# Retention's group norm in a hybrid trunk: roots on compact token sums, outputs in the banks of w_out's last token tile

## The chip, the cores and the metric

One NeuronCore of a Trainium2 chip runs the whole program. The metric is the device time of one execution in microseconds (us); three executions of the kernel before are given, and one more was profiled.

## The reference

The program is one inference step of a two-layer trunk over 384 tokens: 128 prompt tokens and 256 sample tokens, width 1024. Each layer normalises and modulates its input, runs four mixers beside each other (retention, Hyena, windowed attention, latent attention) on one combined input projection, joins their outputs with `w_out`, normalises again, and then runs a gated MLP. All matrices are float32.

What the change touches is the end of the retention mixer and the start of the product with `w_out`:

```python
o = o_f + jnp.flip(o_b, 2)                       # per head: 64 values for each token
mu = jnp.mean(o, axis=-1, keepdims=True)
var = jnp.var(o, axis=-1, keepdims=True)
o = ((o - mu) * lax.rsqrt(var + EPS)).transpose(0, 2, 1, 3).reshape(b, seq_len, RET_WIDTH)
y = jax.nn.silu(gate.astype(jnp.float32)) * (o * gn_g.astype(jnp.float32))
...
y = jnp.concatenate([y_ret, y_hy, y_gqa, y_mla], axis=-1) @ p['w_out']
```

Four heads of 64 channels make 256 channels. Each token has one root per head, so 384 x 4 roots are needed per layer.

## The kernel before

**Layout.** Activations lie with channels on partitions and tokens on the free axis. The 384 tokens are three tiles of 128: tile 0 is the prompt, tiles 1 and 2 the samples. Retention works on two pairs of heads (`pr` = 0, 1); a pair fills 128 partitions, 64 for each head. Wide products are made in three passes: each float32 operand is cut into a rounded upper part (ACT, line 355) and a lower part (DVE, or GpSimd where `eng=G` is given, line 356), and upper x upper, upper x lower and lower x upper are summed in one bank. These passes are the lines 1236 to 1238 for `w_out`.

**PSUM.** There are eight banks: two of tag "a", five of tag "m", one of tag "n". A bank is given to a tile when the planner places its first instruction, and passes on when all users of the tile before are done.

**Retention's tail** (`retention`, lines 1190 to 1226), for each pair: scores of samples against samples into two "a" banks (line 1196), times the decay tables (`W`, line 1199), then the outputs `o` of all 384 tokens into one "a" bank (lines 1204, 1207, 1211). Values and states were made mean-free before, so `o` has mean zero and only its variance is left. It is squared on ACT (1214), summed over the 64 channels of each head and spread back to all 128 partitions by one product with the block matrix `bd` into a second "a" bank `rvp` (1216). The root (ACT, 1217), the reciprocal and one Newton step (DVE, 1218 to 1221) work on 128 x 384 values, in which each root stands 64 times. Then DVE multiplies by the gate (1223) and by `o` and the gain `gn` (1224), and the result is cut into upper and lower parts (`mix`). The second pair needs both "a" banks for its scores, and these are held by the first pair's `o` and `rvp`.

**The product with w_out.** `acc` has six banks: three token tiles times two halves of 512 columns. `mixout[k]`, k = 0 to 7, are the eight 128-channel slices of the mixers' outputs; k = 0 and 1 are retention's two pairs. The weights of k = 6, 7, 4 are multiplied first for all three tiles (18 matmuls for each k). The weights of k = 5, 2, 3 go into the same three buffers (`wh`) that hold those of 6, 7, 4, so each is cut when an earlier one has been read for the last time; those of k = 0, 1 and of the MLP's first two units `up_w` have buffers of their own (`wq`). Then `out_part(t, h)`, steps `ma` and `mb` of token tile t, adds k = 5, 2, 3 for both halves (18 matmuls) and k = 0, 1 for half h (6 matmuls). Steps `q`, `y`, `b`, `r`, `n`, `x` are the norm and residual of a tile, `s` to `i` the next norm, the transposes (`ta`, `tv`, line 759) and the modulation. Their order on PE, DVE and ACT is written out by hand in `OUT_ORDER` (first layer) and `OUT_LAST_ORDER` (second layer, where `tv0` stands ahead of `ma2`).

**What sets the order around the change.** Retention and the early part of `w_out` aren't ordered by hand on PE, DVE and ACT: a planner with a cost for each instruction simulates the engines and puts the earliest in the program's order that is ready next. On the chip each engine then runs that fixed order. On SP the block's loads keep their order: weights of k = 6, 7, 4, 5, 2, 3, 0, 1, then `up_w`, then the gates `gg`; other loads, such as those of `x`, may be placed between. A weight load needs one of five `raw` buffers, which is free when both parts have been cut from it.

Of the kernel before, what the change touches and what calls it, by code (L numbers as in the profile page):

```python
# [9 lines left out]
F32 = mybir.dt.float32  # L10
# [4 lines left out]
ALU = mybir.AluOpType  # L15
# [69 lines left out]
def _consts():  # L85
    p = np.arange(128)
    c0, c, cf = {}, {}, {}
    c0["ident"] = np.eye(128)
    perm = np.zeros((128, 128))
    perm[p ^ 32, p] = 1.0  # L90
    c["perm"] = perm
    c["iup"] = np.broadcast_to(np.arange(1, 257)[None], (128, 256))
    cos, sin = _rope(256, 64)
    c["rc"] = np.tile(np.concatenate([cos, cos], 1).T, (2, 1))
    c["rs"] = np.tile(np.concatenate([-sin, sin], 1).T, (2, 1))
    cos, sin = _rope(256, 32)
    mt = np.zeros((128, 256))
    mt[64:96] = np.concatenate([cos, cos], 1).T
    mt[96:128] = np.concatenate([-sin, sin], 1).T
    c["mrope"] = mt  # L100
    kc = np.concatenate([cos, cos], 1).reshape(2, 128, 32).transpose(1, 0, 2)
    ks = np.concatenate([-sin, sin], 1).reshape(2, 128, 32).transpose(1, 0, 2)
    c["kc"] = kc.reshape(128, 64)
    c["ks"] = ks.reshape(128, 64)
    w256 = (2 * np.arange(256) + 1) * np.pi / 512
    w128 = (2 * np.arange(128) + 1) * np.pi / 256
    a = np.outer(p + 0.5, w256)
    c["fc"] = np.cos(a)
    c["fs"] = -np.sin(a)
    c["ic"] = np.cos(a).T.reshape(2, 128, 128).transpose(1, 0, 2).reshape(128, 256)  # L110
    c["is"] = np.sin(a).T.reshape(2, 128, 128).transpose(1, 0, 2).reshape(128, 256)
    a = np.outer(p, w128)
    c["pfc"] = np.cos(a)
    c["pfs"] = -np.sin(a)
    c["bd"] = np.where(p[:, None] // 64 == p[None, :] // 64, 1.0 / 64, 0.0)
    c["pic"] = np.cos(a).T
    c["pis"] = -np.sin(a).T
    m0 = np.where(p[None, :] <= p[:, None], 0.0, -1e30)
    m1 = np.where(p[None, :] >= p[:, None], 0.0, -1e30)
    zs, ts = _zfeat(256)  # L120
    zp, tp = _zfeat(128)
    col = np.zeros((128, 16))
    col[:, 0:3] = np.stack([-tp, -ts[:128], -ts[128:]], 1)
    for b, (w, L) in enumerate(((w256[:128], 256), (w256[128:], 256), (w128, 128))):
        col[:, 3 + 3 * b] = np.cos(w / 2) / L
        col[:, 4 + 3 * b] = np.sin(w / 2) / L
        col[:, 5 + 3 * b] = -np.cos(w / 2) / L
    col[:, 12] = 127 - p
    col[:, 13] = p
    col[:, 14] = EPS  # L130
    c0["col"] = col
    a3 = np.zeros((128, 3))
    a3[64:, 0] = 1.0
    a3[:64, 2] = 1.0
    c0["addc"] = a3
    m = np.arange(256)
    a = np.outer(m + 0.5, w256)
    cf["gc"] = np.cos(a).reshape(2, 128, 256).transpose(1, 0, 2).reshape(128, 512)
    cf["gs"] = np.sin(a).reshape(2, 128, 256).transpose(1, 0, 2).reshape(128, 512)
    a = np.outer(p + 0.5, w128)  # L140
    cf["gpc"] = np.cos(a)
    cf["gps"] = np.sin(a)
    z = np.zeros((17, 384))
    z[:, 0:128] = zp.T
    z[:, 128:384] = zs.T
    return c0, c, cf, {"z": z, "mask": np.concatenate([m0, m1], 1), "lag": np.arange(384)[None, :] - 128 - p[:, None]}
# [122 lines left out]
def trunk(ctx: ExitStack, tc: tile.TileContext, A, O, offs, depth=DEPTH):  # L269
# [76 lines left out]
    def bank(tag="a", name="bk"):  # L346
        kw = {"bufs": 1} if tag == "n" else {}
        return (pa if tag == "a" else pm).tile([128, 512], F32, tag=tag, name=name, **kw)
# [771 lines left out]
    def retention(l, mx, M, P_, rt, hi, lo, tma):  # L1120
# [8 lines left out]
        for src, dst, n in ((v4, vcn.rearrange("p t (h e) -> p t h e", h=4), 12), (s0, s0c.rearrange("p (a e) -> p a e", a=4), 4)):  # L1129
            mu = sm.tile([128, 12], F32, tag="rmu", name="rmu", bufs=1)[:, 0:n]  # L1130
            m = mu.rearrange("p (t h) -> p t h", t=3) if n == 12 else mu
            V.tensor_reduce(out=m, in_=src, op=ALU.add, axis=AX.X)
            V.tensor_scalar(mu, mu, 1.0 / 64, None, ALU.mult)
            V.tensor_tensor(out=dst, in0=src, in1=m.unsqueeze(3 if n == 12 else 2).to_broadcast(list(dst.shape)), op=ALU.subtract)
        q, k, sg = [], [], []
        for j in range(6):
            ps = fm_proj(l, 9 + j, hi, lo)
# [3 lines left out]
                (q if j < 2 else k).append(f)  # L1141
            else:
                th = mx.tile([128, TP], F32, tag="w15", name="rth", bufs=11)
                S.activation(out=f, in_=ps[:, 0:TP], func=ACTF.Copy, scale=0.5)
                S.activation(out=th, in_=ps[:, 0:TP], func=ACTF.Tanh, scale=0.5)
                V.scalar_tensor_tensor(out=f, in0=th, scalar=1.0, in1=f, op0=ALU.add, op1=ALU.mult)
                sg.append(f)
# [38 lines left out]
            W0.append(M(("wuk", "wuv")[b]).rearrange("p (a c) -> p a c", a=2))  # L1186
            V.tensor_tensor(out=W0[b], in0=pc[b][:, 0:256].rearrange("p (a c) -> p a c", a=2), in1=tabs[:, :, b, 128:256], op=ALU.mult)
        s4 = s0c.rearrange("p (a b e) -> p a b e", a=2, b=2)
        gn = P_("gn")
        for pr in range(2):  # L1190
            sc = [bank("a", "rsc") for _ in range(2)]
            W = [mx.tile([128, 2, 256], F32, tag="PT", name="rW", bufs=3) for _ in range(2)]
# [4 lines left out]
            for b in range(2):  # L1197
                for j in range(2):
                    V.tensor_tensor(out=W[b][:, j], in0=sc[b][:, 256 * j:256 * j + 256],
                                    in1=tab[:, 2 * pr + b, 128 - 128 * j:384 - 128 * j], op=ALU.mult)  # L1200
            o = bank("a", "rob")
            hs = [slice(64 * (2 * pr + b), 64 * (2 * pr + b) + 64) for b in range(2)]
            for b in range(2):
                T.matmul(o[64 * b:64 * b + 64, 0:128], vcn[:, 0, hs[b]], W0[b][:, pr], start=True, stop=True)
# [5 lines left out]
                    r = slice(64 * b, 64 * b + 64)  # L1210
                    T.matmul(o[r, 128:384], s4[r, pr, dr], qd[r, pr, dr], start=False, stop=(dr == 1))

            sq, y, u = (mx.tile([128, 384], F32, tag="w15", name=n, bufs=11) for n in ("rsq", "rya", "ru"))
            S.activation(out=sq, in_=o[:, 0:384], func=ACTF.Square)
            vp = bank("a", "rvp")[:, 0:384]
            T.matmul(vp, cc("bd"), sq, start=True, stop=True)
            S.activation(out=y, in_=vp, func=ACTF.Sqrt, bias=col(14))
            V.reciprocal(y, y)
            V.tensor_tensor(out=u, in0=y, in1=y, op=ALU.mult)
            V.scalar_tensor_tensor(out=u, in0=vp, scalar=EPS, in1=u, op0=ALU.add, op1=ALU.mult)  # L1220
            V.scalar_tensor_tensor(out=y, in0=u, scalar=-3.0, in1=y, op0=ALU.add, op1=ALU.mult)
            for x0, x1, g0 in ((0, 128, 0), (128, 384, 130)):
                V.scalar_tensor_tensor(out=y[:, x0:x1], in0=y[:, x0:x1], scalar=-0.5, in1=sg[pr][:, g0:g0 + x1 - x0], op0=ALU.mult, op1=ALU.mult)
            V.scalar_tensor_tensor(out=y, in0=o[:, 0:384], scalar=gn[:, pr:pr + 1], in1=y, op0=ALU.mult, op1=ALU.mult)
            a, b_ = mix_tiles(pr)
            split(y, a[:, 0:384], b_[:, 0:384])

# [91 lines left out]
    for l in range(depth):  # L1319
# [4 lines left out]
        with ExitStack() as ph:  # L1324
# [76 lines left out]
            wqc = tc.tile_pool(name="wq", reuse_waits="tile", bufs=4, side="right")  # L1401
            wq = wqc.__enter__()
            gg = gate_tiles(wq)
            acc = banks6("acc")
            with tc.manual_schedule(engines={mybir.EngineType.SP}):
                for j, k in enumerate((6, 7, 4)):
                    down_step(acc, wunit(A["wout"][l, k]), mixout[k], T0, j == 0, False)
                ws = [(wunit(A["wout"][l, k]), mixout[k]) for k in (5, 2, 3)]
                ws += [(wunit(A["wout"][l, k], 1024, wq), mixout[k]) for k in (0, 1)]
                up_w = [wunit(A["wup"][l, u], 1024, wq, eng=G) for u in (0, NF)]  # L1410
                for r in range(2):
                    gate_load(gg, 2 * (l % 2), r)
        vec1, vec2 = vecs[l, 1], vecs[l, 2]
# [147 lines left out]
```

## Time and profile before

| | us |
|---|---|
| median of 3 runs | 1109.37 |
| lowest, highest | 1106.87, 1114.67 |
| the profiled execution's own time | 1114.31 |
| its span in the trace | 1112.5 |

| engine | busy us | share |
|---|---|---|
| PE | 1083.0 | 97% |
| PEld (weight loads, beside PE) | 899.1 | 81% |
| DVE | 676.0 | 61% |
| ACT | 499.9 | 45% |
| POOL | 75.3 | 7% |

PE is TensorE, DVE is VectorE, ACT is ScalarE, POOL is GpSimd, SP issues the DMAs. A timeline row gives the start in us from the span's start, the duration in us, the engine, the line, the operation with what it writes and reads, its shape, how many were merged, and in brackets the idle time before it with what ended it. The busy time of a PE row includes the pipeline's end, so the spacing of matmuls is read from their starts. A row of the chain of waits has start, us, and the instruction. The mean granted clock of the whole run is 0.987 of TensorE's full 2.4 GHz.

### The profile page before, as it was taken

To read this page: it belongs to the slowest core of one execution; us is meant where nothing else is said; L and a number is where in the kernel's file an instruction comes from. 1 tells how busy PE (TensorE), PEld (TensorE's weight loads), DVE (VectorE), ACT (ScalarE), POOL (GpSimd) and SP (SyncE) were. 2 spreads that over 40 slices of the span, in tenths; PEclk is the share of its full clock that TensorE was granted. 3 is DMA by queue.
4 is the path that set the end of the run, shared out by engine and by line. 5 is a ranking of instruction groups with operands and counts; after the bars stand their busy time and mean duration, and the time that the engine had idled before them with its cause. 6 is when DMAs were issued, how large, how long until landed. Compare 5 with 4: busy or idle time off the path is not lost.

```text
span 1112.5 us, 15627 instructions
## 1 busy us (share of the span) xinstructions
PE 1083.0 (97%) x5779; PEld 899.1 (81%) x5779; DVE 676.0 (61%) x1465; ACT 499.9 (45%) x1099; POOL 75.3 (7%) x82
## 2 busy tenths in 40 slices
PE   9999999997899999999999999999799999999997
PEld 3596767665699999999987786787589999999996
DVE  6858954477785545455565666658666454554554
ACT  6655534242764433334465544533366343343433
POOL 3210000002200000000002000001220000000000
PEclk9999999998999999999999999999889999999999
DMA  9765345856555333334337615461616434333301
GB/s 348 239 247 163 133 151 201 301 203 227 190 198 169 133 133 114 133 114 132 110 122 244 231 65 183 162 218 42 207 51 198 147 117 131 116 124 131 125 19 57
DMA packets 53017, 176.12 MB, mean 158 GB/s; under 512 B 8618, under 2 KB 10538, under 8 KB 52429
## 3 DMA queue, kind: packets, MB, share of 16 engines
q1 hardware_dynamic: 49229, 171.26, 44.9%
q10 hardware_dynamic: 3712, 3.87, 1.0%
q8 instruction: 45, 0.74, 0.3%
q14 instruction: 31, 0.25, 0.1%
HBM read 169.66 MB, written 5.44 MB: 157 GB/s over the span
## 4 chain that ended last, share of the span: by engine, by line
PE 90%; DVE 7%; ACT 2%; issue 1%; DMA 0%; DVEq 0%; ACTq 0%
PE ups L380 6%; PE gps L380 6%; PE gps L382 6%; PE ups L382 6%; PE gps L381 6%; PE ups L381 6%; PE facc L1236 5%; PE facc L1238 5%; PE facc L1237 5%; PE adaps L404 4%; PE fmps L380 4%; PE fmps L382 4%; PE fmps L381 4%; PE acc L1236 2%; PE acc L1237 2%; PE acc L1238 2%
## 5 line engine op out<-in xcount | busy, mean ns | idle before, releaser
L356 DVE TENSOR_TENSOR wlo<-raw,whi 128x512 fp32r<-128x512 f32 (+2 forms) x380 | 257.2, 706 | 215.7 <-ACT whi L355 215.4
L355 ACT CAST whi<-raw 128x512 fp32r<-128x512 f32 (+2 forms) x388 | 221.4, 610 | 282.6 <-PE gps L381 97.8
L1236 PE MATMUL facc<-whi,fah 128*128 128x512 f32 x264 | 104.5, 396 | 0.5 <-ACT fah L355 0.5
L1237 PE MATMUL facc<-wlo,fah 128*128 128x512 f32 x264 | 103.9, 394 | 0.0
L1238 PE MATMUL facc<-whi,fal 128*128 128x512 f32 x264 | 103.8, 395 | 0.0
L380 PE MATMUL gps<-hTa,whi 128*128 128x386 f32 (+4 forms) x184 | 62.4, 339 | 0.0
L380 PE MATMUL ups<-hTa,whi 128*128 128x386 f32 (+4 forms) x184 | 62.3, 339 | 0.0
L380 PE MATMUL gps<-hTb,whi 128*128 128x386 f32 (+4 forms) x184 | 62.3, 339 | 0.0
L380 PE MATMUL ups<-hTb,whi 128*128 128x386 f32 (+4 forms) x184 | 61.6, 335 | 0.6 <-ACT hTb L772 0.6
L381 PE MATMUL ups<-hTb,whi 128*128 128x386 f32 (+4 forms) x184 | 61.4, 334 | 0.8 <-POOL hTb L775 0.8
L382 PE MATMUL gps<-hTa,wlo 128*128 128x386 f32 (+4 forms) x184 | 62.1, 337 | 0.0
L381 PE MATMUL ups<-hTa,whi 128*128 128x386 f32 (+4 forms) x184 | 61.9, 336 | 0.0
L381 PE MATMUL gps<-hTa,whi 128*128 128x386 f32 (+4 forms) x184 | 61.9, 336 | 0.0
L381 PE MATMUL gps<-hTb,whi 128*128 128x386 f32 (+4 forms) x184 | 61.8, 336 | 0.0
L382 PE MATMUL gps<-hTb,wlo 128*128 128x386 f32 (+4 forms) x184 | 61.8, 336 | 0.0
L382 PE MATMUL ups<-hTa,wlo 128*128 128x386 f32 (+4 forms) x184 | 61.8, 336 | 0.0
L382 PE MATMUL ups<-hTb,wlo 128*128 128x386 f32 (+4 forms) x184 | 61.5, 334 | 0.0
L404 PE MATMUL adaps<-araw,cs 128*32 128x512 f32 x384 | 60.2, 602 | 0.0
L1238 PEld LDWEIGHTS facc<-whi,fal 128*128 128x128 f32 x264 | 49.6, 188 | 11.9
L1236 PEld LDWEIGHTS facc<-whi,fah 128*128 128x128 f32 x264 | 49.6, 188 | 10.8 <-ACT fah L355 0.9
L1237 PEld LDWEIGHTS facc<-wlo,fah 128*128 128x128 f32 x264 | 49.6, 188 | 9.9
L1236 PE MATMUL acc<-whi,mix 128*128 128x512 f32 x96 | 41.1, 434 | 11.8 <-ACT mix L355 11.8
(366 smaller groups left out, 2340.9 us busy)
## 6 DMA issues: line engine op xcount, KB each, us to landing
araw<-in_ada_dram SPq DMA_DIRECT2D x96, 512.0 KB, 4.4
raw<-in_wup_dram SPq DMA_DIRECT2D x88, 512.0 KB, 3.3
raw<-in_wdn_dram SPq DMA_DIRECT2D x44, 512.0 KB, 3.2
raw<-in_win_dram SPq DMA_DIRECT2D x30, 512.0 KB, 4.4
raw<-in_wout_dram SPq DMA_DIRECT2D x16, 512.0 KB, 5.2
gg<-gd SPq DMA_DIRECT2D x8, 512.0 KB, 5.8
raw<-in_wta_dram SPq DMA_DIRECT2D x8, 416.0 KB, 3.3
x<-in_x_dram SPq DMA_DIRECT2D x6, 512.0 KB, 6.7
```

Source lines behind the costliest of these rows:

```text
L355: S.copy(hi, src)
L356: (eng or V).tensor_tensor(out=lo, in0=src, in1=hi, op=ALU.subtract)
L380: T.matmul(out, ah, bh, start=start, stop=False)
L381: T.matmul(out, ah, bl, start=False, stop=False)
L382: T.matmul(out, al, bh, start=False, stop=stop)
L404: T.matmul(self.ps[32 * j:32 * j + 32, :], cs[:, k, :], rows[j // 2][:, 512 * (j % 2):512 * (j % 2) + 512], start=(k == self.k0), stop=(k ...
L1236: T.matmul(acc[t][h], ah[:, cs_], wh_[:, hs], start=first, stop=False)
L1237: T.matmul(acc[t][h], ah[:, cs_], wl_[:, hs], start=False, stop=False)
L1238: T.matmul(acc[t][h], al[:, cs_], wh_[:, hs], start=False, stop=last)
```

## The change

Retention: the gain `gn` is folded into the gate's scale (`gnh`). A Sqrt on a dummy column (`sqrt_table`) stands ahead of the pairs. `o` moves from an "a" to an "m" bank. Per pair, three products with the squares as stationary operand and the two columns of `two` as moving operand give each token's two sums, with tokens on partitions, in columns 384 to 389 of `o`'s own bank; `rstd` makes root, reciprocal and Newton step on 128 x 6 values. After both pairs a second loop spreads the roots back: six products per pair of a root column, read 64 times over, with the identity, into an "a" bank, and then DVE multiplies by the gate and by `o`. The matrix `bd` of 128 columns goes, `two` has 2.

w_out: of the five "m" banks that `acc` takes, the last two go to token tile 2, and tile 1 has one "m" and the "n" bank. The early k = 6, 7, 4 are multiplied for tiles 0 and 1 first, and then all three for tile 2. The lower parts of `up_w` are cut on DVE where GpSimd did it.

```diff
-    c["bd"] = np.where(p[:, None] // 64 == p[None, :] // 64, 1.0 / 64, 0.0)
+    c["two"] = np.where(p[:, None] // 64 == np.arange(2)[None, :], 1.0, 0.0)
...
+        gnh = sm.tile([128, 2], F32, tag="rgn", name="rgn", bufs=1)
+        V.tensor_scalar(gnh, P_("gn"), 0.5, None, ALU.mult)
...
-                S.activation(out=f, in_=ps[:, 0:TP], func=ACTF.Copy, scale=0.5)
+                S.activation(out=f, in_=ps[:, 0:TP], func=ACTF.Copy, scale=gnh[:, j - 4:j - 3])
...
-        gn = P_("gn")
+        sqrt_table(qd[:, 1, 1, 0:1])
+        outs = []
         for pr in range(2):
...
-            o = bank("a", "rob")
+            o = bank("m", "rob")
...
-            sq, y, u = (mx.tile([128, 384], F32, tag="w15", name=n, bufs=11) for n in ("rsq", "rya", "ru"))
+            sq, y = (mx.tile([128, 384], F32, tag="w15", name=n, bufs=11) for n in ("rsq", "ry"))
             S.activation(out=sq, in_=o[:, 0:384], func=ACTF.Square)
-            vp = bank("a", "rvp")[:, 0:384]
-            T.matmul(vp, cc("bd"), sq, start=True, stop=True)
-            S.activation(out=y, in_=vp, func=ACTF.Sqrt, bias=col(14))
-            V.reciprocal(y, y)
-            V.tensor_tensor(out=u, in0=y, in1=y, op=ALU.mult)
-            V.scalar_tensor_tensor(out=u, in0=vp, scalar=EPS, in1=u, op0=ALU.add, op1=ALU.mult)
-            V.scalar_tensor_tensor(out=y, in0=u, scalar=-3.0, in1=y, op0=ALU.add, op1=ALU.mult)
+            for t in range(3):
+                T.matmul(o[:, 384 + 2 * t:386 + 2 * t], sq[:, 128 * t:128 * t + 128], cc("two"), start=True, stop=True)
+            outs.append((o, y, rstd(o[:, 384:390], 6, 64)))
+        for pr in range(2):
+            o, y, rs = outs[pr]
+            rb = bank("a", "rrb")
+            for t in range(3):
+                for b in range(2):
+                    T.matmul(rb[64 * b:64 * b + 64, 128 * t:128 * t + 128], rs[:, 2 * t + b:2 * t + b + 1].to_broadcast([128, 64]),
+                             ident, start=True, stop=True)
             for x0, x1, g0 in ((0, 128, 0), (128, 384, 130)):
-                V.scalar_tensor_tensor(out=y[:, x0:x1], in0=y[:, x0:x1], scalar=-0.5, in1=sg[pr][:, g0:g0 + x1 - x0], op0=ALU.mult, op1=ALU.mult)
-            V.scalar_tensor_tensor(out=y, in0=o[:, 0:384], scalar=gn[:, pr:pr + 1], in1=y, op0=ALU.mult, op1=ALU.mult)
+                V.tensor_tensor(out=y[:, x0:x1], in0=rb[:, x0:x1], in1=sg[pr][:, g0:g0 + x1 - x0], op=ALU.mult)
+            V.tensor_tensor(out=y, in0=o[:, 0:384], in1=y, op=ALU.mult)
             a, b_ = mix_tiles(pr)
             split(y, a[:, 0:384], b_[:, 0:384])
...
-            acc = banks6("acc")
+            b6 = [bank("m" if i < 5 else "n", "acc") for i in range(6)]
+            acc = [b6[0:2], [b6[2], b6[5]], b6[3:5]]
             with tc.manual_schedule(engines={mybir.EngineType.SP}):
-                for j, k in enumerate((6, 7, 4)):
-                    down_step(acc, wunit(A["wout"][l, k]), mixout[k], T0, j == 0, False)
+                early = [(wunit(A["wout"][l, k]), mixout[k]) for k in (6, 7, 4)]
+                for ts in ((0, 1), (2,)):
+                    for j, e in enumerate(early):
+                        down_step(acc, *e, T0, j == 0, False, ts)
...
-                up_w = [wunit(A["wup"][l, u], 1024, wq, eng=G) for u in (0, NF)]
+                up_w = [wunit(A["wup"][l, u], 1024, wq) for u in (0, NF)]
```

The helper that both kernels have and the change now calls for the roots:

```python
    def rstd(ss, n, d):
        ...
        S.activation(out=y, in_=ss, func=ACTF.Sqrt, scale=1.0 / d, bias=col(14))
        V.tensor_scalar(b, ss, -0.5 / d, -0.5 * EPS, ALU.mult, ALU.add)
        V.reciprocal(y, y)
        V.tensor_tensor(out=u, in0=y, in1=y, op=ALU.mult)
        V.tensor_tensor(out=u, in0=u, in1=b, op=ALU.mult)
        V.scalar_tensor_tensor(out=y, in0=u, scalar=1.5, in1=y, op0=ALU.add, op1=ALU.mult)
        return y
```

## Rows read from the trace of the kernel before

**Rows 1.** Page, part 4: shares of the chain that ended last, by engine.
```profile
PE 90%; DVE 7%; ACT 2%; issue 1%; DMA 0%; DVEq 0%; ACTq 0%
```

**Rows 2.** Waits of PE, whole span: us in total, times, longest us.
```profile
PE acc L1236 <- ACT mix L355: 11.8, 2, 6.2
```

**Rows 3.** PE timeline, the end of PE's work ahead of each wait, and after.
```profile
262.86 0.40 PE L1237 MATMUL acc<-wlo,mix 128*128 128x512 f32 x1
263.09 0.40 PE L1238 MATMUL acc<-whi,mix 128*128 128x512 f32 x1
269.14 0.80 PE L1236 MATMUL acc<-whi,mix 128*128 128x512 f32 x1 [5.66 <-ACT mix L355]
...
273.93 0.39 PE L1238 MATMUL acc<-whi,mix 128*128 128x512 f32 x1
...
787.03 0.40 PE L1238 MATMUL acc<-whi,mix 128*128 128x512 f32 x1
793.62 0.80 PE L1236 MATMUL acc<-whi,mix 128*128 128x512 f32 x1 [6.19 <-ACT mix L355]
...
799.64 0.40 PE L1238 MATMUL acc<-whi,mix 128*128 128x512 f32 x1
```

**Rows 4.** Stretch after the second wait: PE to POOL busy, PEclk, DMA share, GB/s.
```profile
793.70:800.00 6.30, 6.30 (x16) 4.96 (x17) 2.39 (x8) 1.96 (x6) 0.00 (x0) 0.54 0.44 180
```

**Rows 5.** DVE timeline, first layer, from the first pair's W to the last multiplication.
```profile
238.60 0.75 DVE L1199 TENSOR_TENSOR rW<-rsc,tab 128x256 f32<-128x256 f32 x2
...
251.50 0.69 DVE L356 TENSOR_TENSOR wlo<-raw,whi 128x512 fp32r<-128x512 f32 x1
...
252.97 0.61 DVE L1224 SCALAR_TENSOR_TENSOR rya<-rob,lp,rya 128x384 f32<-128x384 f32 x1
...
256.73 6.18 DVE L356 TENSOR_TENSOR wlo<-raw,whi 128x512 fp32r<-128x512 f32 x4
262.84 2.54 DVE L1218 RECIPROCAL rya<-rya 128x384 f32<-128x384 f32 x1
...
267.93 0.62 DVE L1224 SCALAR_TENSOR_TENSOR rya<-rob,lp,rya 128x384 f32<-128x384 f32 x1
```

**Rows 6.** PE timeline, first layer, the second pair's scores and last outputs.
```profile
250.98 1.13 PE L1196 MATMUL rsc<-rf,rf 64*128 64x256 f32 x4
...
254.56 1.13 PE L1196 MATMUL rsc<-rf,rf 64*128 64x256 f32 x4
...
258.52 1.08 PE L1211 MATMUL rob<-rpack,lm 64*64 64x256 f32 x8
```

**Rows 7.** Chain of waits, first layer: start us, us, what.
```profile
228.27 0.59 PE rst L1171 x8
...
243.25 0.65 PE rvp L1216 x2
...
286.17 0.44 PE tps L759 x4
```

**Rows 8.** DVE timeline: a Newton operation on one column.
```profile
275.48 0.16 DVE L718 SCALAR_TENSOR_TENSOR rz<-rz 128x1 f32<-128x1 f32 x1
```

**Rows 9.** POOL timeline, the lower parts of up_w.
```profile
255.88 6.48 POOL L356 TENSOR_TENSOR wlo<-raw,whi 128x512 fp32r<-128x512 f32 x4 [21.30 <-ACT whi L355]
```

**Rows 10.** ACT timeline: the Sqrt table's load; the first square of tile 0.
```profile
243.98 1.28 ACT L1217 ACT_TABLE_LOAD   x1 [1.08 <-PE rvp L1216]
...
795.30 0.60 ACT L703 ACTIVATE sqj<-acc 128x512 bf16<-128x512 f32 x1 [1.74 <-PE acc L1238]
```

**Rows 11.** PE timeline: the first matmul after a 128*64 group; tile 0's transposes.
```profile
242.29 0.50 PE L1237 MATMUL acc<-wlo,mix 128*128 128x512 f32 x1
...
805.45 0.60 PE L759 MATMUL tps<-cst,xn 128*128 128x128 f32 x4
805.80 0.48 PE L1236 MATMUL acc<-whi,mix 128*128 128x512 f32 x1
```

**Rows 12.** SP timeline, second layer: the loads of x.
```profile
788.27 1.46 SPq L309 DMA_DIRECT2D x<-xd  x3
```

## Prediction

> **What bounds the kernel now.** I read the chain of waits first: PE carries 90% of it [rows 1], so a change is worth what it takes out of PE's stream or adds to it. The list of PE's waits comes next. There the largest entry by far is `acc` waiting for `mix` from ACT: 11.8 us in two waits, one per layer [rows 2]. The timeline shows each: PE stands still between the matmul that starts at 263.09 and the one at 269.14, and again from 787.03 to 793.62 [rows 3]. Matmuls of this kind start 0.23 apart (262.86, 263.09), so the waits cost 269.14 - 263.09 - 0.23 = 5.82 and 793.62 - 787.03 - 0.23 = 6.36 us. After each, PE is slow: in the stretch after the second the granted clock is 0.54 [rows 4], so mostly the 1.2 GHz level. The first layer has 11 starts from 269.14 to 273.93, which take 4.79 us where 11 x 0.232 = 2.55 would do; the second has 14 from 793.62 to 799.64, 6.02 us for 3.25 [rows 3]. That is 2.24 + 2.77 = 5.01 us more. So 17.2 us, 1.5% of the run, hang on these two waits.
>
> What PE waits for is the second pair of retention. In the first layer the decayed scores `W` of the first pair are done at 239.35, but the second pair's scores run only at 250.98 and 254.56 [rows 5, 6]: they need the two "a" banks that the first pair's `rvp` and `o` hold, and `o` is read for the last time at 252.97 to 253.58 [rows 5]. From there the chain is serial: outputs until 259.6 [rows 6], a reciprocal over 384 columns of 2.54 us, which itself stands behind four weight cuts (6.18 us), and the last multiplication ends at 268.55 [rows 5]. The second layer repeats this 524 us later.
>
> **The change part by part.**
>
> *Banks.* With `o` in an "m" bank and no `rvp`, the second pair's scores wait only for the first pair's `W`, so they can start near 239.4. From the second score group to the end of the last multiplication it takes 268.55 - 254.56 = 14.0 us now [rows 5, 6]. Both groups together last about 2.2 us [rows 6], so even at this length the end comes at 239.35 + 1.1 + 14.0 = 254.5. It should be shorter: from the reciprocal's start to the last multiplication's it takes 267.93 - 262.84 = 5.1 us now, and five small operations (0.16 each [rows 8], some 1.0 with gaps), the spreading (0.9, below) and two multiplications stand there instead, some 2.7; and the four cuts of 6.18 us lie beside GpSimd's own cuts of 6.48 us [rows 9], while one cut alone takes 0.69 [rows 5]. I estimate 250 to 254.5.
>
> *Order of w_out.* The early matmuls are 54 (three k, 18 each); tile 2's 18 now stand behind the retention outputs' release, and so do tile 0's 18 for k = 5, 2, 3 (their buffers come free only when tile 2 has read the early weights) and the 3 of k = 0. That takes 39 x 0.232 = 9.05 us of cover away ahead of the wait. PE, dense up to 263.32 now, would reach tile 2's first matmul at 263.32 - 9.05 + 2.2 (added work, below) = 256.5, which is 2 to 6.5 us after the banks come free. Behind it the same 9.05 us cover the cast of `mix` and the cuts of k = 5, 2, 3 (each 2 x 0.69 on DVE after 18/3 = 6 matmuls or 1.4 us of PE work). So I take both waits as gone: 5.82 + 6.36 = 12.2 us. Of the slow matmuls' 5.01 us I count half, 2.5: they lie beside tile 0's norm on ACT and DVE, which sets part of the stage's end.
>
> *PE work.* Per pair `rvp` goes (0.65 [rows 7]). The three sums issue 6 instructions (a float32 product is two passes, as in rvp's x2) that load 128 x 128 weights for two columns. No row shows that; the bounds are `rst`'s 0.59/8 = 0.074 and `rvp`'s own 0.325 each, the nearest are the transposes, 0.44/4 = 0.11 with weights of the same size [rows 7]: 0.66. Spreading back is 12 instructions of 64 weight columns and 128 moving ones, like `rst`: 12 x 0.074 = 0.89 (upper bound 12 x 0.11 = 1.32). Going to another kind of matmul and back costs some 0.1 (the first `acc` after a group takes 0.50 [rows 11], the others 0.40 [rows 3]), once more each way: 0.2. Net 0.66 + 0.89 + 0.2 - 0.65 = 1.1 per pair, 2.2 per layer, 4.4 in all; with the bounds 2.7 to 12.
>
> The spreading uses half-width column tiles. The Trainium skill, TensorEngine Tiling (Array Packing), Key Properties, says that changing the tiling mode drains TensorE, which speaks against the change. The trace shows little of it: the first `acc` behind a 128*64 group takes 0.50, behind full-width transposes 0.48 [rows 11]. If each of 8 added mode changes cost a full 0.40 instead, the gain below would be some 2.4 us smaller.
>
> *DVE, ACT, POOL, SP.* DVE loses over 2 us per pair (the 2.54 of the reciprocal alone) and gains four cuts (4 x 0.69 = 2.8 per layer); POOL's 6.48 go. I cost this at nothing, since DVE is idle beside PE there; without that cover it would be 2.8 per layer. The cuts of `up_w` come later now (their `raw` buffer is k = 5's) and may fall into tile 0's norm. In the second layer tile 0's transposes stand ahead of `ma2`; now they start at 805.45, 10.15 after tile 0's first square at 795.30 [rows 10, 11]. PE will be there 6.36 + 2.77 - 2.2 = 6.9 earlier, at 798.5; the square moves to about 787.26 + 2.2 + 0.7 = 790.2, and 10.15 later is 800.35. So a new wait of 0 to 1.9 us; I take 1. The gain in the gate's scale is one tiny DVE operation per layer, the Sqrt table's load (1.28 [rows 10]) moves to idle ACT time: nothing, at worst one or two more loads there. The loads of `x` (788.27 [rows 12]) are issued after retention's last matmuls; these come earlier, so the loads can too.
>
> *Sum.* 12.2 + 2.5 - 4.4 - 1 = 9.3 us less. The profiled execution took 1114.31 (span 1112.5 and 1.8 around it) and would take 1105.0. It lies 4.9 above the median of 1109.37, against which I forecast 1100.
>
> **Rivals.**
>
> *More is won.* All of the slow matmuls' time comes back, the added PE work is at its lower bound, no new wait: 17.2 - 2.7 = 14.5, hence 1095. For it: nothing but PE bounds most of the stage. Against: tile 0's norm. Chance 0.12.
>
> *The wait moves to tile 0's norm.* The cuts of k = 5, 2, 3 and of `up_w`, or late gates, hold tile 0 back, and PE stands at `tv0` in the second layer, or between tile 2's early matmuls and `ma0`, 2 to 3 us per layer, and goes slow again. Then about half is left, 4 to 5 us: 1105. For it: weights, `raw` buffers and gates now hang on tile 2's early matmuls. Against: 9 us of cover. Chance 0.18.
>
> *Slower: less cover ahead of an unchanged chain.* The planner, or DVE's and ACT's fixed order, may leave the second pair where it is. PE then stands at tile 2's early matmuls with 39 matmuls still to come. From a release later than 269.14 - 9.05 = 260.1 in the first layer (784.6 in the second) every us costs one; at the old chain's 268.55 it is 8.5 per layer, 17 in all: 1126; at 263, 6: 1115. Against: the second pair's scores wait for nothing but banks. Chance 0.09.
>
> *It does not do what it says.* Another tile takes the freed banks and the wait stays, the added work being covered by it: 1109. Chance 0.05.
>
> **How the numbers follow.** The forecast has the remaining 0.56, with its own range 1095 to 1105 from the bounds of the PE work and of the clock's share. A measurement of this kernel tells about 1% from no change: below 1098.3 counts as faster, above 1120.5 as slower. Of the forecast's 0.56, 0.22 lie below 1098.3. Faster: 0.22 + 0.12 = 0.34. Slower: 0.07 of the third rival's 0.09. Within: 0.34 + 0.18 + 0.05 + 0.02 = 0.59. The range of 8 in 10 holds the forecast, the gain's lower half and no change: 1093 to 1110.
>
> **What would show it.** Right: no wait of PE on `mix` over 1 us between retention and `ma0`; the second pair's scores within 3 us of the first pair's `W`; clock 1.00 there; spreading at about 0.9 us per pair. Wrong: PE waiting on DVE's last multiplication at tile 2's early matmuls, on a weight cut ahead of `ma0`, or on `xn` at `tv0`; sums of 0.3 us per instruction.

## The result, and the profile after

The changed kernel takes 1096.15 us in the median of four runs (1093.04 to 1096.46), the kernel before 1111.65 in the four runs beside it (1106.87 to 1114.67): a ratio of 0.986, with a 95% interval of 0.981 to 0.990. So 15.5 us are gone, where the forecast had 9.3, and its 1100 stands 3.9 us too high.

The profiled execution after took 1093.04, 21.3 less than the one before (1114.31). To see how much of that is the change, I measure one stretch in both: from retention's first `rst` product to the MLP's first `ups` product, which holds all that the diff touches behind the gate except one line, the dummy root (its own section below). PE's timeline of after, columns as in the rows ahead of the prediction:

```profile
225.80 0.66 PE L1173 MATMUL rst<-rpack 128*64 128x128 f32 x8
...
283.80 0.36 PE L380 MATMUL ups<-hTb,whi 128*128 128x258 f32 x1 [0.57 <-ACT hTb L772]
...
739.17 0.66 PE L1173 MATMUL rst<-rpack 128*64 128x128 f32 x8
...
797.87 0.31 PE L380 MATMUL ups<-hTb,whi 128*128 128x130 f32 x1
```

The same four rows of before:

```profile
228.20 0.66 PE L1171 MATMUL rst<-rpack 128*64 128x128 f32 x8
...
292.59 0.36 PE L380 MATMUL ups<-hTb,whi 128*128 128x258 f32 x1 [0.56 <-ACT hTb L772]
...
747.25 0.66 PE L1171 MATMUL rst<-rpack 128*64 128x128 f32 x8
...
815.06 0.31 PE L380 MATMUL ups<-hTb,whi 128*128 128x130 f32 x1
```

The stretch falls from 64.39 to 58.00 in the first layer and from 67.81 to 58.70 in the second: 6.39 + 9.11 = 15.50 us. That the medians give the same to the hundredth is chance: in the runs below a difference of medians and one of stages lie up to 2.4 us apart. I call this sum of two stretches **the stage** (132.20 before, 116.70 after) and give it for each experiment. The other 5.8 us between the two profiled executions are not the change's; the last section shows the largest piece.

What PE waits for, over the whole span of after (us in total, times, longest us):

```profile
PE tps L759 <- DVE xn L752: 4.5, 3, 2.0
...
```

The entry of 11.8 us [rows 2] is gone, and nothing has come in its place. The chain that ended last is now, by engine:

```profile
PE 91%; DVE 5%; ACT 1%; issue 1%; DMA 0%; POOL 0%; DVEq 0%; ACTq 0%; POOLq 0%
```

DVE's share fell from 7% [rows 1]. Retention's tail after, first layer, on PE, with the last multiplication on DVE (two views, the DVE row alone in the second fence):

```profile
234.32 0.70 PE L1199 MATMUL rsc<-rf,rf 64*128 64x256 f32 x2
...
239.00 1.13 PE L1199 MATMUL rsc<-rf,rf 64*128 64x256 f32 x4
...
245.12 0.73 PE L1220 MATMUL rob<-cst,rsq 128*128 128x2 f32 x6
245.70 0.48 PE L1244 MATMUL acc<-wlo,mix 128*128 128x512 f32 x1
246.02 0.39 PE L1245 MATMUL acc<-whi,mix 128*128 128x512 f32 x1
...
247.03 1.53 PE L1227 MATMUL rrb<-cst,ry 128*64 128x128 f32 x24
248.49 0.50 PE L1243 MATMUL acc<-whi,mix 128*128 128x512 f32 x1
248.83 0.39 PE L1244 MATMUL acc<-wlo,mix 128*128 128x512 f32 x1
...
253.47 0.40 PE L1243 MATMUL acc<-whi,mix 128*128 128x512 f32 x1
```

```profile
250.68 0.55 DVE L1231 TENSOR_TENSOR ry<-rob,ry 128x384 f32<-128x384 f32 x1
```

The second pair's scores run at 234.32 to 239.00, not at 250.98 and 254.56 [rows 6]; the outputs are read for the last time at 251.23 (268.55 before [rows 5]); the 37th `w_out` matmul of the layer, tile 2's first, starts at 253.47 and waits for nothing. In the second layer it is closer: read by 770.24, and tile 2's second half begins at 770.87. The clock, where it was 0.54 [rows 4] (a stretch of after, second layer; busy us of PE, PEld, DVE, ACT, POOL, then PEclk, DMA share, GB/s):

```profile
772.00:780.00 8.00, 8.00 (x36) 6.46 (x35) 5.00 (x8) 4.13 (x8) 0.00 (x0) 1.00 1.02 368
```

### The profile page after: what moved, and what is told of

The parts are those of the page before. It is cut to its first block, busy times and chain, and to the rows that moved or that the text cites. A ratio compares the mean times of both kernels' runs of the same rounds, so it can differ in the third digit from the quotient of the medians.

```text
span 1091.2 us, 15755 instructions
## 1 busy us (share of the span) xinstructions
PE 1072.9 (98%) x5843; PEld 892.9 (82%) x5843; DVE 658.5 (60%) x1479; ACT 504.6 (46%) x1105; POOL 62.0 (6%) x74
## 4 chain that ended last, share of the span: by engine, by line
PE 91%; DVE 5%; ACT 1%; issue 1%; DMA 0%; POOL 0%; DVEq 0%; ACTq 0%; POOLq 0%
PE ups L380 6%; PE gps L380 6%; PE ups L382 6%; PE gps L381 6%; PE gps L382 6%; PE ups L381 6%; PE facc L1243 5%; PE facc L1245 5%; PE facc L1244 5%; PE adaps L404 4%; PE fmps L380 4%; PE fmps L382 4%; PE fmps L381 3%; PE acc L1243 2%; PE acc L1244 2%; PE acc L1245 2%
## 5 line engine op out<-in xcount | busy, mean ns | idle before, releaser
L356 DVE TENSOR_TENSOR wlo<-raw,whi 128x512 fp32r<-128x512 f32 (+2 forms) x388 | 254.3, 686 | 220.8 <-ACT whi L355 220.6
L1259 ACT ACTIVATE fth<-fc 128x386 f32<-128x386 f32 x44 | 23.2, 528 | 55.1 <-DVE fc L1258 55.0
```

Of the source, the lines that this page charges most:

```text
L356: (eng or V).tensor_tensor(out=lo, in0=src, in1=hi, op=ALU.subtract)
L1259: S.activation(out=th, in_=c, func=ACTF.Tanh)
```

## The experiments

The kernel before ran beside each group. The stage is read from one profile of each kernel. "Ratio" is to it, with its 95% interval.

| kernel | us, median | before beside it | ratio | stage, us |
|---|---|---|---|---|
| changed kernel again | 1098.53 | 1112.77 | 0.987 [0.985, 0.989] | 116.47 |
| banks and order only | 1105.45 | 1112.77 | 0.994 [0.992, 0.995] | 127.24 |
| roots only | 1097.88 | 1112.77 | 0.987 [0.985, 0.989] | 118.18 |
| before, wait filled, 13 products | 1119.16 | 1112.77 | 1.005 [1.003, 1.007] | 137.39 |
| before, wait filled, 7 products | 1107.08 | 1111.60 | 0.995 [0.993, 0.998] | 127.66 |
| changed, old `w_out` order | 1096.50 | 1111.60 | 0.984 [0.982, 0.987] | 116.35 |
| changed, spread twice | 1098.10 | 1111.60 | 0.987 [0.984, 0.989] | 119.03 |
| changed, full-width spreading | 1095.72 | 1111.60 | 0.984 [0.981, 0.986] | 116.15 |
| before, `up_w` cut on DVE | 1113.00 | 1113.62 | 1.001 [0.998, 1.003] | 130.94 |
| changed, `up_w` cut on GpSimd | 1098.79 | 1113.62 | 0.989 [0.986, 0.992] | 118.74 |
| changed, no dummy root | 1097.10 | 1113.62 | 0.987 [0.984, 0.990] | 116.73 |

### The changed kernel again

> The changed kernel again, unchanged, beside the next three. Every theory expects about 15 us less than the kernel before (1111.65 to 1096.15 in the medians so far). Beside the medians its trace is asked one thing: the profiled execution of the kernel before had a stretch at half the granted clock at 164.6 (3.41 us long), ahead of anything that was changed, and one at 819.96 (10.24 us). If the change had ended the second one, no profile of the changed kernel should show it; if it is chance, either of the two kernels may show or lack it.

14.2 us less than the kernel before, with the same stage (116.47, 116.70 in the first profile). Its profile does have a stretch at half the granted clock, from 808.19 for 6.83 us, at the place where the profile before had one: that stretch isn't a mark of either kernel.

### Banks and order without the roots

Against the changed kernel, the main lines:

```diff
-            for t in range(3):
-                T.matmul(o[:, 384 + 2 * t:386 + 2 * t], sq[:, 128 * t:128 * t + 128], cc("two"), start=True, stop=True)
-            outs.append((o, y, rstd(o[:, 384:390], 6, 64)))
+            outs.append(o)
...
+            vp = bank("a", "rvp")[:, 0:384]
+            T.matmul(vp, cc("bd"), sq, start=True, stop=True)
+            S.activation(out=y, in_=vp, func=ACTF.Sqrt, bias=col(14))
+            V.reciprocal(y, y)
...
```

> Banks and order without the compact roots: the outputs of both pairs lie in m banks, w_out's tile 2 is multiplied behind tiles 0 and 1, but the norm is the old one (product with the block matrix, root, reciprocal and Newton step on 128 x 384 values). Theory A (the moved bank lets the second pair's scores start behind the first pair's W, and that alone removes the waits): the second pair's scores start near 235 in the first layer, no wait of PE for mix over 1 us, and PE work even smaller than after the change, by 2 x 0.65 for the two old products against 1.5 + 1.6 for spreading and sums, 1.8 per layer; so 1092 to 1097. Theory B (the short roots remove the waits): two reciprocals of 2.54 us and the 384-column steps are still in series, the release of the banks comes 5 us or more later per layer than after the change, PE stands for it at tile 2's early matmuls, 3 to 6 us per layer, and falls to the lower clock again: 1105 to 1112.

This is what theory B expected, at the lower edge of its range: 7.3 us less than before in the medians, 5.0 in the stage, so a third to a half of the change. The waits of PE (same columns as above):

```profile
PE acc L1241 <- DVE rya L1229: 8.1, 4, 4.5
...
```

PE now waits for the last multiplications, at tile 2's early matmuls: 8.1 us in four waits, where before it was 11.8 in two, and in both layers the granted clock falls to 0.50 there (257.0 to 263.7 and 779.2 to 782.6). The second pair's scores do run early (236.05 to 240.73), but its outputs, complete at 245.30, are released only at 259.68. PE's, DVE's and ACT's timeline of this kernel show why:

```profile
244.22 1.08 PE L1212 MATMUL rob<-rpack,lm 64*64 64x256 f32 x8
...
249.93 0.81 PE L1221 MATMUL rvp<-rsq,cst 128*128 128x384 f32 x2
...
259.74 0.80 PE L1241 MATMUL acc<-whi,mix 128*128 128x512 f32 x1 [1.16 <-DVE rya L1229]
```

```profile
245.27 2.55 DVE L1223 RECIPROCAL rya<-rya 128x384 f32<-128x384 f32 x1 [0.21 <-ACT rya L1222]
...
251.39 2.55 DVE L1223 RECIPROCAL rya<-rya 128x384 f32<-128x384 f32 x1 [0.84 <-ACT rya L1222]
...
254.80 0.61 DVE L1229 SCALAR_TENSOR_TENSOR rya<-rob,lp,rya 128x384 f32<-128x384 f32 x1
...
259.07 0.61 DVE L1229 SCALAR_TENSOR_TENSOR rya<-rob,lp,rya 128x384 f32<-128x384 f32 x1
```

```profile
247.60 0.48 ACT L1219 ACTIVATE rsq<-rob 128x384 f32<-128x384 f32 x1
```

From the last outputs to the last multiplication's start it is 259.07 - 245.30 = 13.8 us; in the kernel before, where the pairs follow each other, 267.93 - 259.60 = 8.3 [rows 5, 6]. About half of the 5.5 us more lies behind the second pair's reciprocal: both pairs' 384-column norms now share DVE, and the first pair's steps and weight cuts stand between (7.7 us to the last multiplication, 5.1 before). The other half lies ahead of it (6.1 us, 3.2 before). DVE works on the first pair there until 250.55, and the second pair's square on ACT comes only at 247.60, behind a weight cast that waits 1.84 for its DMA, its product on PE only at 249.93. In the profiles' own times the start moves 14.3 us forward and the end only 8.9; this profile runs 0.7 us ahead at the first `rst`, so 13.6 and 8.2.

This kernel also has the changed kernel's second loop for the norms and its `up_w` cuts on DVE. The moved bank with the old single loop wasn't run.

### Roots without the banks

Against the kernel before:

```diff
             o = bank("a", "rob")
...
-            vp = bank("a", "rvp")[:, 0:384]
-            T.matmul(vp, cc("bd"), sq, start=True, stop=True)
...
+            for t in range(3):
+                T.matmul(o[:, 384 + 2 * t:386 + 2 * t], sq[:, 128 * t:128 * t + 128], cc("two"), start=True, stop=True)
+            rs = rstd(o[:, 384:390], 6, 64)
+            rb = bank("a", "rrb")
...
```

> The compact roots without the moved banks: outputs in an a bank, one loop per pair with its spreading, the old order of w_out, up_w's lower parts on GpSimd. Theory A (the bank): the second pair's scores still wait for the first pair's last reading of its outputs, so they start only some 3 to 5 us earlier than before (near 247 in place of 250.98), the chain behind them is some 3 us shorter, and of the waits of 5.8 and 6.4 us up to 2 remain or nothing at all with the old cover of 54 matmuls; the added PE work of 3 to 4 us is there in any case: 1100 to 1108. Theory B (the roots): both waits are gone by the shorter chain alone, and the time equals that of the changed kernel, 1096 to 1098. If the time is at or above that of the kernel before, the roots by themselves are a loss.

Theory B's number: 14.9 us less, as the changed kernel on the same chip (14.2). No wait for `mix` is left; of retention there is only this:

```profile
...
PE rrb L1223 <- DVE ry L338: 0.8, 2, 0.5
```

The second pair still stands behind the first one's outputs, as expected: its scores run at 246.65 and 248.13. But the chain behind is short enough. DVE's timeline, then PE's:

```profile
254.87 0.17 DVE L335 RECIPROCAL ry<-ry 128x6 f32<-128x6 f32 x1
...
258.25 0.56 DVE L1227 TENSOR_TENSOR ry<-rob,ry 128x384 f32<-128x384 f32 x1
```

```profile
248.13 1.13 PE L1198 MATMUL rsc<-rf,rf 64*128 64x256 f32 x4
...
251.89 1.08 PE L1213 MATMUL rob<-rpack,lm 64*64 64x256 f32 x8
...
263.62 0.40 PE L1239 MATMUL acc<-whi,mix 128*128 128x512 f32 x1
```

A reciprocal of 0.17 stands for 2.54 [rows 5]. That helps twice. This profile runs 2.35 us ahead at the first `rst`; counted from there the second pair's outputs are complete 4.3 us earlier (252.97 here, 259.60 [rows 6]), since the first pair's shorter chain frees the banks sooner, and from them to the last multiplication's start it is 5.3 us, not 8.3. The last multiplication starts at 258.25, ACT's cast of the upper part ends at 259.98, and the matmul that needs it comes at 263.62. So 3.6 us are to spare in the first layer. In the second the last multiplication ends at 777.98 and the need is at 780.00. With the old bank, the old order and all 54 early matmuls as cover the wait is gone.

### The wait filled with products of zeros

In the kernel before:

```diff
+                    if t == 0 and h == 0 and j == 4:
+                        for _ in range(13):
+                            T.matmul(acc[0][0], ident, zero8[:, 0:1].to_broadcast([128, 512]), start=False, stop=False)
```

> The kernel before, with 13 float32 products of the identity with zeros (26 instructions of 512 columns, about 5.6 to 6 us) put on PE just ahead of each wait for mix; they add zero to the first acc bank. The wait's end is set by the chain on ACT and DVE and stays; PE is busy while it lasts. So what changes is the granted clock behind the wait alone. Slow matmuls cost 5.0 us of PE's stream in the profile before. If all of that sets the end of the stage: 1106 to 1107 against 1111.65, and the granted clock behind the wait is 1.00. If half of it lies beside tile 0's norm, as the forecast took: 1109. If the clock falls all the same, or the stage's end is set elsewhere: 1111 to 1113.

Slower by 6.4 us, since I had the products' length wrong (PE's timeline):

```profile
265.27 11.37 PE L1429 MATMUL acc<-zero,cst 128*128 128x512 f32 x26
276.07 0.79 PE L1236 MATMUL acc<-whi,mix 128*128 128x512 f32 x1
```

26 instructions take 10.80, 0.415 each, not the 0.23 of `acc`. The fill is 5 us longer than the wait. The clock behind it is 1.00. From the first matmul after the fill to `ups` it is 1.86 and 2.36 us shorter than before. The next kernel has 7 products in place of 13:

> The kernel before with 7 float32 products of zeros in place of 13 ahead of each wait: 14 instructions at the 0.416 us that the 26 took in the run before (11.37 with the pipeline's end, 10.81 from start to next start), 5.8 us, which is the wait's own length (5.82 and 6.36). The chain on ACT and DVE stays, PE is busy while it lasts. In the run with 13 products the stretch from the first slow matmul to the MLP's first product took 1.83 and 2.43 us less than before, 4.3 of 5.0. If that holds here: no wait of PE for mix over 1 us, granted clock 1.00 behind it, and 1107 to 1109 against 1112.8. If the forecast's half was right: 1110. If the fill only replaced idle time and nothing comes back: 1112 to 1114.

```profile
784.23 6.19 PE L1429 MATMUL acc<-zero,cst 128*128 128x512 f32 x14
790.58 0.50 PE L1236 MATMUL acc<-whi,mix 128*128 128x512 f32 x1 [0.16 <-ACT mix L355]
...
791.51 0.40 PE L1236 MATMUL acc<-whi,mix 128*128 128x512 f32 x1
```

Of the waits 0.16 is left, their time is filled and not saved, and the stretch behind the second runs at full clock, like that behind the first:

```profile
789.00:795.00 6.00, 5.84 (x22) 3.76 (x21) 3.12 (x10) 2.48 (x7) 0.00 (x0) 1.00 0.71 288
```

The time falls by 4.5 us in the medians, the stage by 4.54. Of the 5.01 that the slow matmuls cost, nine tenths come back. The missing 0.5 stands right behind the fills: the first three steps take 791.51 - 790.58 = 0.93 in either layer, three plain ones 0.70. So the lower level behind a wait was paid in full, not half hidden beside tile 0's norm.

### The old order of w_out in the changed kernel

```diff
...
-            acc = [b6[0:2], [b6[2], b6[5]], b6[3:5]]
+            acc = banks6("acc")
...
-                for ts in ((0, 1), (2,)):
-                    for j, e in enumerate(early):
-                        down_step(acc, *e, T0, j == 0, False, ts)
+                for j, k in enumerate((6, 7, 4)):
+                    down_step(acc, wunit(A["wout"][l, k]), mixout[k], T0, j == 0, False)
```

> The changed kernel with the old order of w_out's early part (k by k over all three token tiles) and the old share of banks; compact roots and outputs in m banks stay. Two of the six halves now lie in the outputs' banks, one of tile 1 and one of tile 2. If the compact roots are what counts, the chain ends 6 us or more ahead of the need either way and nothing changes: 1097 to 1099, within 1 us of the changed kernel. If the cover order counts (theory C: tile 2 behind the other tiles is what keeps PE busy until the outputs are read): PE stands at the half that waits for the outputs, 2 to 4 us per layer, 1102 to 1106.

The stage is 116.35, as with the new order; no wait of PE appears. Theory C falls: with the compact roots the outputs are read early enough for either order. What the order is worth with the old norm wasn't run.

### Spreading twice, and spreading in full width

```diff
-            for t in range(3):
+            for t in range(6):
+                t = t // 2
```

> The changed kernel with the spreading products done twice; the second pass writes the same values again. The trace of the changed kernel shows both pairs' 24 instructions between starts 247.03 and 248.49, 1.46 us per layer. If PE bounds the stage (the sum counts every added instruction on PE at its full length): 2.9 us more than the changed kernel, 1099 to 1101.5. If part of PE's work there lies beside something else: less than 1 us more. This gives what the change itself pays for spreading, 0.73 per pair against the forecast's 0.89 and the old product's 0.65.

PE's timeline, first layer:

```profile
248.38 2.84 PE L1228 MATMUL rrb<-cst,ry 128*64 128x128 f32 x48
251.16 0.50 PE L1244 MATMUL acc<-whi,mix 128*128 128x512 f32 x1
```

48 instructions take 251.16 - 248.38 = 2.78 from start to start, where 24 take 1.46; both layers together, 2.63 are added. The stage grows by 2.33 over the first profile of the changed kernel and by 2.56 over the second. So nine tenths or more of each us that is added on PE here is paid.

```diff
+            w2 = mx.tile([128, 3, 128], F32, tag="w15", name="rw2", bufs=11)
+            V.tensor_copy(w2.rearrange("p t (b c) -> p (t b) c", b=2), rs.unsqueeze(2).to_broadcast([128, 6, 64]))
             for t in range(3):
-                for b in range(2):
-                    T.matmul(rb[64 * b:64 * b + 64, 128 * t:128 * t + 128], rs[:, 2 * t + b:2 * t + b + 1].to_broadcast([128, 64]), ident, start=True, stop=True)
+                T.matmul(rb[:, 128 * t:128 * t + 128], w2[:, t], ident, start=True, stop=True)
```

> The changed kernel with the spreading in full-width products: DVE first copies each root 64 times into 128 columns (one added operation of 128 x 384 per pair, about 0.55 us, on an engine with time to spare), and 3 products per pair of 128 x 128 weights take the place of 6 with half-width column tiles. By rows (a float32 transpose of that size takes 0.11, six instructions per pair 0.66 against 0.73): 0 to 0.4 us less in all, no difference that can be measured. The Trainium skill, TensorEngine Tiling (Array Packing), Key Properties, says that changing the tiling mode drains TensorE; by that rule the two mode changes per layer that go here would show as a first acc behind the spreading that takes well under the 0.50 of a group behind half-width tiles, and 1 to 2 us less in all.

PE's timeline of the first pair's spreading in full width:

```profile
248.98 0.83 PE L1228 MATMUL rrb<-cst,rw 128*128 128x128 f32 x6
249.57 0.48 PE L1246 MATMUL acc<-whi,mix 128*128 128x512 f32 x1
249.89 0.40 PE L1244 MATMUL acc<-whi,mix 128*128 128x512 f32 x1
```

0.59 for a pair against 0.73, and the first `acc` behind it takes 249.89 - 249.57 = 0.32 to the next start; behind the half-width tiles it is 248.83 - 248.49 = 0.34. The total isn't measurably different. The Trainium skill, TensorEngine Tiling (Array Packing), Key Properties, has a change of tiling mode drain TensorE; in these rows half-width tiles cost 0.02 more than full-width ones at the return to `acc`, so the trace shows no drain of a size that counts here.

### Who cuts up_w

```diff
-                up_w = [wunit(A["wup"][l, u], 1024, wq, eng=G) for u in (0, NF)]
+                up_w = [wunit(A["wup"][l, u], 1024, wq) for u in (0, NF)]
```

This line alone, in the kernel before:

> The kernel before with up_w's lower parts cut on DVE, as the change does; nothing else. In the profile before, DVE's four cuts ahead of the second pair's reciprocal take 6.18 us beside GpSimd's four of 6.48, while four without GpSimd beside them took 2.49 (in the run with the banks alone). If that crowding holds the second pair back: six cuts of 0.62 now stand ahead of the reciprocal, 3.7 us, so it starts about 1 us earlier, but two more cuts of 0.62 stand between it and the last multiplication; net 0 to 1 us less per layer, and the waits of PE for mix stay at 5 to 7 us: 1110 to 1113 beside 1112. If the crowding is a large part of the wait: waits down to 3 to 4 us per layer, 1105 to 1108.

```profile
254.73 3.69 DVE L356 TENSOR_TENSOR wlo<-raw,whi 128x512 fp32r<-128x512 f32 x6
259.79 2.55 DVE L1218 RECIPROCAL rya<-rya 128x384 f32<-128x384 f32 x1 [1.38 <-ACT rya L1217]
```

```profile
PE acc L1236 <- ACT mix L355: 12.2, 2, 6.7
```

Without GpSimd beside them DVE's cuts take 3.69 / 6 = 0.62 in place of 6.18 / 4 = 1.54 [rows 5]; but then DVE waits 1.38 for the root, two cuts stand behind the reciprocal, and PE's waits are as long as before. The four cuts that the forecast saw ahead of the reciprocal held it back by little: in the kernel before the root ends on ACT at 261.76 and the reciprocal starts at 262.84 [rows 5], 1.1 us later (0.4 in the second layer). The Trainium skill, SBUF — State Buffer, Who interferes with whom, has DVE and GpSimd share a port pair that only one of them holds at a time; cuts that take 0.62 alone and 1.54 beside GpSimd's agree with that. In the changed kernel, the other way round (`eng=G` put back):

> The changed kernel with up_w's lower parts cut on GpSimd, as before the change. The forecast costed the move of these cuts at nothing. If that holds: within 1 us of the changed kernel, 1095 to 1099, PE's waits unchanged. If GpSimd's cuts crowd DVE's cuts of k = 5, 2, 3 here (1.54 each in place of 0.62, as in the profile before), these come too late for tile 0: PE waits for a weight cut ahead of tile 0's second part, 1 to 4 us per layer, 1098 to 1105, and the move of the cuts is a needed part of the change.

```profile
PE acc L1244 <- DVE wlo L356: 1.3, 3, 0.6
```

PE now waits three times for a weight cut, 1.3 us; from start to start, with the slower step behind each, the three cost 2.1, and the stage is 2.0 longer. The medians' intervals (0.986 to 0.992 here, 0.981 to 0.990 for the change) don't separate the two; the trace does.

### No dummy root

```diff
-        sqrt_table(qd[:, 1, 1, 0:1])
```

> The changed kernel without the root on a dummy column ahead of the pairs. In the changed kernel's trace a table load of 1.28 us stands directly ahead of the first pair's root all the same (239.63 in the first layer, 761.35 in the second), so taking the dummy out changes nothing there: within 1 us of the changed kernel, and the trace shows the same load at the same place. If the dummy did save a load on the chain, the banks would come free 1.3 us later; in the second layer they are free at 770.24 and PE reaches tile 2's second half at 770.9, so PE would wait about 0.6 us there.

Same stage, same load. ACT's timeline of this kernel:

```profile
242.22 1.28 ACT L333 ACT_TABLE_LOAD   x1
```

The changed kernel has it too, at 239.63, dummy or not. So the line buys nothing. It even adds loads, because the planner puts the dummy far ahead of the pairs, before a Tanh of the gate (line 1147). The changed kernel's ACT timeline, second layer:

```profile
715.32 1.28 ACT L344 ACT_TABLE_LOAD   x1
...
732.43 1.28 ACT L1147 ACT_TABLE_LOAD   x1
```

Line 344 is the dummy. Neither of the two loads is in the run without it, and the first layer has two more (187.17 and 206.12): 18 loads in the changed kernel, 14 without the dummy and 14 in the kernel before. They cost nothing that the stage or the medians show.

## Why the prediction was right, and where not

The measured 1096.15 lies near the lower end of the forecast's own range, 1095 to 1105. Its sum was 12.2 + 2.5 - 4.4 - 1 = 9.3; the first term held, and the other three were each too cautious, by 2.5, 2.7 and 1. So it also falls below 1098.3, which the forecast called faster and gave a chance of 0.34.

**Waits gone, 12.2.** Held in full: nothing waits for `mix` or for the outputs' banks.

**Slow matmuls, half of 5.01.** Mis-sized. The run with the wait filled shows 4.5 coming back, and the other 0.5 taken by the return from the fill. The forecast thought tile 0's norm would hide half; it doesn't.

**Added PE work, 4.4 net.** The single prices were near. A pair's sums push the `acc` matmuls around them back by 0.68 (the second behind them starts at 246.02, where two steps of 0.23 from the last one ahead, at 244.88, give 245.34), forecast 0.66. Spreading takes 1.46 / 2 = 0.73 a pair and some 0.1 for the changes of kind, forecast 0.89 and 0.2. `rvp`'s removal gives 0.65 back, as forecast: 0.35 for itself (260.34 to 260.69) and 0.30 for the step of `acc` behind it, which takes 0.53 (before):

```profile
260.69 0.69 PE L1238 MATMUL acc<-whi,mix 128*128 128x512 f32 x1
261.22 0.40 PE L1236 MATMUL acc<-whi,mix 128*128 128x512 f32 x1
```

What the sum put at nothing is the second pair's scores, which no longer come late. In the second layer eight of them now start in as much time as four did (before, then after):

```profile
776.52 1.13 PE L1196 MATMUL rsc<-rf,rf 64*128 64x256 f32 x4
```

```profile
749.52 1.13 PE L1199 MATMUL rsc<-rf,rf 64*128 64x256 f32 x8
```

Counting PE's time from start to start by tile, both layers, each with the slower `acc` steps beside it: outputs with sums +2.82, spreading +3.33, `rvp` -2.59, scores -2.29 (of which -1.52 in the second layer's scores themselves), the rest +0.42. Net 1.7, below the forecast's lower bound of 2.7. The scores' part comes from where the planner put them, and nobody had priced it: as far as the forecast goes, that is luck.

**New wait at tile 0's transposes, 1.** None came; the waits on `xn` are 4.5 in three in every profile. The 10.15 us that the forecast took from tile 0's square to its transposes are PE's own: no idle time stands before the transposes at 805.45 [rows 11], and `xn` was ready at 803.89, 8.6 after the square. After the change `xn` is ready at 787.53, 7.4 after the square, and the transposes start at 788.27.

The sum with these sizes is 12.2 + 5.0 - 1.7 = 15.5, which is the stage's gain; the 1.7 and the slow clock's 5.0 are read from the same two profiles, so this is a breakdown and not a second measurement. The rival "more is won" (1095) came nearer than the forecast's 1100, by its first and third conditions and a PE price even under its lower bound.

**DVE and the cuts, nothing.** Right for the change as made; but the cuts' move is part of why: put back on GpSimd they cost 2.0.

**The reason was weighted wrongly.** The forecast explained the gain by the banks: the second pair starts early, "even at this length the end comes at 239.35 + 1.1 + 14.0 = 254.5", and the short roots were an extra. The runs say the reverse. Banks and order alone leave 8.1 us of waits, and the end comes at 259.68. That step of the forecast moved a chain of 14.0 us forward as if nothing else ran on its engines; there it takes 259.68 - 240.73 = 19.0, since the two long norms meet on DVE, and ACT and PE have other work ahead of the second pair's. Roots alone remove all of the waits for `mix`. Together they do little more than the roots: the stage is 1.5 to 1.7 us shorter than with the roots alone, which still cut `up_w` on GpSimd, and the medians don't differ. With the compact roots the order of `w_out`, which the forecast spent most care on, changes nothing that can be measured. Its picture of that order was good, though: in the clock of before (this profile runs 2.4 us ahead there) PE reaches tile 2 at 255.9 and the banks are free at 253.6; forecast 256.5 and 250 to 254.5.

No version tried beats the changed kernel by more than the measurement can tell; the roots alone reach its time with a smaller edit.

## What to carry to other kernels

When a chain ends later than the work that needs it, price its removal from both ends: what moves its start, and what shortens it. A start moved forward makes chains overlap, and two long chains on one engine give part of it back; a chain shortened at its costliest operation (here 384 columns in which each root stood 64 times) gave nothing back here, and where two chains follow each other it also lets the second start sooner. Where PE bounds the stage, a wait that is followed by a stretch at the lower clock costs that stretch as well, so put it into the sum whole.

## What the runs showed of the hardware

A stretch at half the granted clock comes in some executions and not in others behind the same work. In every profile PE stands about 2 us for `xn` ahead of the second layer's last transposes. Stretches behind that place, in the first and then in the second profile of the changed kernel, which runs 4.0 us later there:

```profile
805.00:810.00 5.00, 4.78 (x45) 4.54 (x45) 1.21 (x2) 4.70 (x11) 3.54 (x3) 1.00 0.01 3
```

```profile
810.00:815.00 5.00, 5.00 (x25) 5.00 (x25) 1.99 (x3) 4.97 (x12) 3.48 (x3) 0.50 0.01 3
```

The clock fell there in 7 of the 13 profiles, of both kinds of kernel, and cost 2.7 to 4.3 us from the first `ups` to the first `facc` (23.0 without it, 25.7 to 27.2 with it). The long waits for `mix`, 5.5 to 6.7 us of idle time, were in contrast followed by the lower level all four times, in both profiles that had them (the kernel before, and with `up_w` cut on DVE). What decides in the shorter case stays open.

A DVE weight cut of 512 columns takes 0.62 in a row of its own kind and, in the kernel before, 1.36 to 1.54 beside GpSimd's cuts. A float32 product of 512 columns takes 0.415 per instruction, one of cut operands 0.23.
